# Score tiles of queries made by transposing DMAs, keys kept as their high part twice, and four moves in the order of a one-core transformer layer

## The chip, the cores and the metric

The kernel runs on one core of a Trainium2 chip. The metric is the device time of one execution in microseconds. The kernel before took 2648.01 us as the median of three runs (2645.45 to 2649.12). The core has five engines that run their own instruction streams in order and wait for each other by semaphores: TensorE (PE, with its weight loads shown apart as PEld), VectorE (DVE), ScalarE (ACT), GpSimd (POOL) and SyncE (SP), which here issues nearly all DMAs.

## The reference, cut to what matters

One layer over 2048 latent tokens of width 1024, with 256 context tokens, in f32:

```python
h = rmsnorm(x, norm1_g) * (1 + sc1) + sh1
rq, rk, rv, rg, aq, ak, av = split(h @ w_in)      # 4 x 512, 512, 128, 128
ret = chunkwise_retention(rope(rq), rope(rk), rv, both directions)
ret = groupnorm(ret) * silu(rg)
q = rope(rmsnorm(aq by heads))                    # 8 heads of 64
k = rope(rmsnorm(ak by heads))                    # 2 heads of 64, context keys ahead
att = softmax(q @ k.T / 8) @ v                    # 4 query heads share a key head
x = x + g1 * (concat(ret, att) @ w_out)
h2 = rmsnorm(x, norm2_g) * (1 + sc2) + sh2
x = x + g2 * (relu(h2 @ w_ff1) ** 2 @ w_ff2)
out = rmsnorm(x, final_norm_g)
```

## The kernel before, in words

Products that need more than f16 are made of three f16 products: each operand is split into a high part and the low rest, and high x high, high x low and low x high are summed in PSUM. A tile of tokens is 128 rows; there are 16 of latents and 2 of context, 18 of keys in all.

**Projection (0 to 603 us).** The list `units` is run through one step s at a time. A step multiplies one tile with one block of columns of `w_in` (lines 1192 to 1194, 24 products of 512 columns), then `run_step(s)` issues what other work was registered for that step by `do(s, part, fn)`, in the fixed order of `PARTS` (line 305): "hi", "evac", "turned", "low", "vec", "pool", "root", "aux", "turn", "load", "store". Work that follows a product is registered for the steps s + 1 to s + 7 (`post`, line 688 ff). Tiles come in two groups: group 0 is the context and latents 0 to 3; group 1 the other twelve. In group 1 the columns of retention keys (RK) and of attention keys and values (AKV) alternate, after them attention queries (AQ) and retention queries (RQ). In the same steps the kernel also reads the weights of later stages (tiles `wm`, `wmo`, `wor`, `wst`), for DVE to sum, scale and split.

A tile of queries is normed and rotated on DVE and POOL into `ys`, turned on PE at s + 4 (line 711: four transposes of 128x128 into the PSUM tile `psx`), its high part made by ACT (line 782) and its low part by DVE (line 785) into `qhl`, and stored at s + 6 to the scratch `aq` (line 789) with the head's dimensions in the partitions. A tile of keys: the rotated key goes into `kn`; ACT makes its high part `kh` (line 829), DVE the low part beside the key (line 832), PE turns both at once (line 837, s + 6), DVE casts the result into `ks` (line 842, s + 7), so `ks` holds the high part in partitions 0 to 63 and the low part in 64 to 127. The PSUM tiles `psx` are shared by these transposes and by those of the latents (line 480).

The latents of group 1 are prepared in group 0's last steps and after (lines 1228 to 1254): load at step b - 4, square on ACT at b - 2, root at b - 1, norm on DVE at b (line 466), then the transposes on PE at b (line 480), then a scale that frees the PSUM tile (line 485).

**Attention (603 to 1458 us).** Iterations k of some 1.48 us, 18 to a group of four query heads of one token tile, 32 groups. In each iteration the events registered by `on(k, phase, fn)` run phase by phase. A group is loaded 14 iterations ahead (`Group.load`, lines 157 to 164, four DMAs into `qr`), its largest scores are found by `piece` (lines 177 and 181) and DVE (line 190), and its scores are two products (lines 210 and 211). `piece` of the first groups runs already within the projection. Retention runs beside it: the forward states are updated chunk by chunk (`update`, line 1643) in two SBUF places of tag "sf", and each is stored (`keep_state`, line 1648). The backward states have two places of tag "sb", used after. `output_scales` (line 1759) finds the scales of the output product; its last eight instructions are registered one to an iteration.

**Feed-forward (1458 to 2647 us).** Jobs of 12 products each (lines 2071 to 2073) of sums of blocks; an item has seven forms of weights `w1f`, made by ACT (line 2047) and DVE (line 2053). The last token tile's remaining work waits in the list `rest`: two groups of four transposes (line 1865), two modulations (line 1870), two shifts (line 1875), two stores. After the products of each job `rest_steps(2)` issues two of them, and once the list is empty its two PSUM banks are given to the jobs.

Of the kernel before, what the change touches and what calls it, by code (L numbers as in the profile page):

```python
# [22 lines left out]
P = 128  # L23
# [33 lines left out]
def layer_kernel(ctx: ExitStack, tc: tile.TileContext, a: dict, out: bass.AP):  # L57
# [34 lines left out]
    aq_d = scratch("aq", NT, [P, 2, 4, P], F16)  # L92
# [56 lines left out]
    class Group:  # L149
# [7 lines left out]
        def load(self):  # L157
            pool, tag = (mq, "mb") if self.n % 4 < 2 else (qp, "qr")
            self.qr = pool.tile([P, 2, 4, P], F16, name="qr", tag=tag, bufs=2)
            q = self.qr.rearrange("p x (j e) t -> p x j e t", e=2)  # L160
            for e in range(2):
                src = aq_d[self.t][64 * e : 64 * e + 64, :, 2 * self.g : 2 * self.g + 2]
                nc.sync.dma_start(q[:64, :, :, e], src)
                nc.sync.dma_start(q[64:, :, :, e], src)
# [105 lines left out]
    with ExitStack() as st, tc.manual_schedule():  # L270
# [418 lines left out]
        def post(s, g, col, kind, i, x):  # L689
# [73 lines left out]
            elif col == C_AQ:  # L763
# [25 lines left out]
                do(s + 6, "store", lambda: nc.sync.dma_start(aq_d[i], x["z"]))  # L789
            else:  # L790
# [36 lines left out]
                def high():  # L827
                    x["kh"] = op.tile([P, 2, HD], F16, name="kh", tag="kh")
                    nc.scalar.activation(x["kh"], x["kn"][:, :, 0], AF.Copy)

                def low():
                    nc.vector.tensor_tensor(x["kn"][:, :, 1], x["kn"][:, :, 0], x["kh"], op=ALU.subtract)
# [9 lines left out]
                do(s + 7, "vec", lambda: nc.vector.tensor_copy(ks[:, :, row * P : (row + 1) * P], x["pt"][:, :2]))  # L842
# [389 lines left out]
        for n, tile_of in enumerate(GROUPS[1]):  # L1232
# [288 lines left out]
    for g in range(2):  # L1521
        nc.sync.dma_start(ks2[:64, g], ks[:64, g])
# [87 lines left out]
    def retention(k0):  # L1610
# [94 lines left out]
        for n, (d, c) in enumerate(todo):  # L1705
# [6 lines left out]
            if d == 0:  # L1712
                old, to, tag = ("f" if c == STATES else "s", c - 2), ("s", c - 1), "sf"
# [45 lines left out]
    def output_scales(k):  # L1759
# [20 lines left out]
        def scales():  # L1780
# [11 lines left out]
            for i, fn in enumerate(later):  # L1792
                on(k + 4 + i, "late", fn)
# [163 lines left out]
    output_scales(39)  # L1957
# [450 lines left out]
    with tc.manual_schedule():  # L2408
# [78 lines left out]
```

## Time and profile before

| | us |
|---|---|
| median of three runs | 2648.01 |
| the profiled execution | 2648.93 |
| its span | 2647.1 |
| PE busy | 2597.4 |
| DVE busy | 2048.4 |
| POOL busy | 1756.4 |
| ACT busy | 1504.0 |

The mean granted clock of TensorE over the execution was 0.997 of full speed. A row of a timeline gives the start and the duration in us, the engine, the line of the kernel, what is written and read, and in brackets how long the engine had idled before and what it waited for. DMA rows on SP show the issue; landing times stand apart.

### The profile page before, as it was taken

What the parts mean: (1) busy time and instruction counts of PE and PEld (TensorE: products, weight loads), DVE (VectorE), ACT (ScalarE), POOL (GpSimd) and SP (SyncE); (2) the same over time, 40 slices, a digit from 0 to 9 for tenths busy, and PEclk for the clock granted to TensorE, in tenths of its full rate; (3) what the DMA queues carried; (4) which work ended last, traced back from release to release, by engine and by line L of the source; (5) the groups of instructions that cost most, each with busy time, mean ns of one, the idle gap of its engine ahead of it and who ended that gap; (6) DMA issues with size and microseconds to landing.
All of it is one profiled execution on the core that took longest, in us unless ns stands there. A gap on an engine that the chain in (4) does not pass through costs nothing.

```text
span 2647.1 us, 45439 instructions
## 1 busy us (share of the span) xinstructions
PE 2597.4 (98%) x16617; PEld 1452.3 (55%) x16617; DVE 2048.4 (77%) x3098; ACT 1504.0 (57%) x2544; POOL 1756.4 (66%) x1451
## 2 busy tenths in 40 slices
PE   8999999998999999999999999999999999999998
PEld 5875555545666666666666444444444444444443
DVE  5788898667888888888887697889886656656686
ACT  3855343426877777888788576666665322222243
POOL 3644566545676668798887685677662666666686
PEclk9999999999999999999999999999999999999999
DMA  7876999737112123333322755777685757475453
GB/s 235 270 253 211 309 325 322 261 116 221 51 57 73 57 85 100 95 85 107 112 81 77 278 160 151 236 237 230 211 291 148 278 174 296 163 288 178 157 189 113
DMA packets 332903, 481.84 MB, mean 182 GB/s; under 512 B 90228, under 2 KB 200068, under 8 KB 328200
## 3 DMA queue, kind: packets, MB, share of 16 engines
q1 hardware_dynamic: 332664, 478.94, 54.9%
q8 instruction: 130, 2.13, 0.3%
q14 instruction: 93, 0.76, 0.1%
q10 hardware_dynamic: 16, 0.01, 0.0%
HBM read 321.89 MB, written 156.38 MB: 181 GB/s over the span
## 4 chain that ended last, share of the span: by engine, by line
PE 82%; DVE 6%; DMA 4%; ACT 4%; issue 2%; POOL 2%; SPq 0%; ACTq 0%; DVEq 0%; POOLq 0%
PE pd L2298 7%; PE pd L2300 7%; PE pd L2299 7%; PE pu L2071 7%; PE pu L2073 7%; PE pu L2072 7%; PE st L210 4%; PE o L245 4%; PE st L211 4%; PE pso L1193 4%; PE pso L1192 4%; PE pso L1194 4%; PE mp L177 3%; PE o L243 2%; PE bank L1835 2%; PE bank L1833 2%
## 5 line engine op out<-in xcount | busy, mean ns | idle before, releaser
L190 DVE TENSOR_REDUCE nm<-mp 128x1 f32<-128x512 f32 x558 | 377.5, 685 | 88.6 <-PE mp L177 82.9
L216 ACT ACTIVATE p<-st 128x512 f32<-128x512 f32 x576 | 341.4, 600 | 158.4 <-PE st L211 154.8
L227 POOL TENSOR_TENSOR plo<-p,phi 128x1024 f16<-128x1024 f32 x160 | 347.7, 2178 | 84.9 <-ACT phi L220 84.8
L2071 PE MATMUL pu<-hf,w1f 128*128 128x512 f16 x896 | 339.8, 379 | 0.6 <-DVE u L1870 0.6
L2072 PE MATMUL pu<-hf,w1f 128*128 128x512 f16 x896 | 339.8, 379 | 0.0
L2073 PE MATMUL pu<-hf,w1f 128*128 128x512 f16 x896 | 339.8, 379 | 0.0
L2298 PE MATMUL pd<-w,uf 128*128 128x512 f16 x896 | 339.6, 379 | 0.0
L2299 PE MATMUL pd<-w,uf 128*128 128x512 f16 x896 | 339.6, 379 | 0.0
L2300 PE MATMUL pd<-w,uf 128*128 128x512 f16 x896 | 339.6, 379 | 0.0
L2318 POOL TENSOR_TENSOR y<-y,d 128x512 f32<-128x512 f32 x128 | 210.4, 1646 | 146.9 <-ACT uf L2287 100.1
L220 ACT ACTIVATE phi<-p 128x1024 f16<-128x1024 f32 x288 | 305.2, 1060 | 0.0
L229 DVE TENSOR_TENSOR plo<-p,phi 128x512 f16<-128x512 f32 x256 | 237.6, 929 | 21.8 <-ACT phi L220 9.4
L243 PE MATMUL o<-wv,plo 128*128 128x65 f16 x2304 | 230.6, 193 | 0.0
L245 PE MATMUL o<-wv,phi 128*128 128x129 f16 x2176 | 228.9, 220 | 0.0
L210 PE MATMUL st<-qr,ks 128*128 128x512 f16 x576 | 218.3, 379 | 10.3 <-ACT p L216 7.9
L243 PEld LDWEIGHTS <-plo 128*128 128x128 f16 x2304 | 205.5, 98 | 29.3 <-issue 1.5
L2310 DVE SCALAR_TENSOR_TENSOR y<-pd,scy,y 128x512 f32<-128x512 f32 x160 | 116.8, 747 | 131.5 <-PE pd L2300 131.5
L211 PE MATMUL st<-qr,ks 128*128 128x512 f16 x576 | 218.5, 379 | 0.0
L2083 DVE TENSOR_TENSOR r<-pu,r 128x512 f32<-128x512 f32 x224 | 149.9, 683 | 82.8 <-PE pu L2073 57.7
L1192 PE MATMUL pso<-wf,h_l 128*128 128x512 f16 (+1 forms) x576 | 208.1, 361 | 0.0
L1194 PE MATMUL pso<-wf,h_l 128*128 128x512 f16 (+1 forms) x576 | 208.1, 361 | 0.0
L1193 PE MATMUL pso<-wf,h_l 128*128 128x512 f16 (+1 forms) x576 | 208.1, 361 | 0.0
(392 smaller groups left out, 6110.4 us busy)
## 6 DMA issues: line engine op xcount, KB each, us to landing
wm<-in_w_ff SPq DMA_DIRECT2D x64, 512.0 KB, 7.1
u<-r SPq DMA_DIRECT2D x128, 256.0 KB, 4.5
ur<-u SPq DMA_DIRECT2D x128, 256.0 KB, 5.8
y<-x SPq DMA_DIRECT2D x64, 512.0 KB, 6.0
wf<-w2f SPq DMA_DIRECT2D x112, 256.0 KB, 3.0
w<-wf SPq DMA_DIRECT2D x28, 1024.0 KB, 10.2
w1r<-in_w_ff SPq DMA_DIRECT2D x48, 512.0 KB, 5.4
x<-y SPq DMA_DIRECT2D x48, 512.0 KB, 2.6
```

What stands on the lines that cost most here:

```text
L190: nc.vector.tensor_reduce(dst, src, axis=AX.X, op=ALU.max, negate=True)
L211: mm(ps, ks2[:, self.g, k], q[:, 1], start=False, stop=True)
L216: nc.scalar.activation(self.p[kt // 2][:, kt % 2], self.s.pop(kt), AF.Exp, scale=HD**-0.5)
L227: nc.gpsimd.tensor_tensor(lo, p, hi, op=ALU.subtract)
L243: mm(o[:, : HD + 1], lo[:, i, c], v[:, : HD + 1], start=False, stop=False)
L245: mm(o, hi[:, i, c], v[:, :VW], start=False, stop=last)
L2071: mm(pu[hf, i], whi, hi, start=k == 0, stop=False)
L2072: mm(pu[hf, i], whi, lo, start=False, stop=False)
L2073: mm(pu[hf, i], wlo, hi, start=False, stop=k == 3)
L2298: mm(ps, u[:, 0, b], w[:, b, 0], start=b == 0, stop=False)
L2299: mm(ps, u[:, 0, b], w[:, b, 1], start=False, stop=False)
L2300: mm(ps, u[:, 1, b], w[:, b, 0], start=False, stop=b == 3)
```

## The change

1. Queries. ACT and DVE split the rotated queries where they lie, token-major in SBUF, and `aq` keeps them so: per head 64 columns of high and 64 of low part. The PE transposes of queries are gone. `Group.load` now issues two transposing DMAs in place of four plain ones.
2. Keys. ACT copies the key beside itself instead of making its high part, and DVE's subtraction before the transposes is gone. After them DVE casts both copies into `ks`, which so holds the high part twice, and subtracts it from the PSUM tile into a new tile `kl` (one buffer). A new store sends `kl` to a scratch; `ks2` is loaded from there.
3. The third forward state is written into a place of tag "sb".
4. `output_scales` begins one iteration sooner, and its last eight instructions go two to an iteration.
5. Latents of group 1 are squared, rooted and normed one step sooner.
6. The list `rest` is started after job 2 instead of after job 0.

```diff
         def load(self):
             pool, tag = (mq, "mb") if self.n % 4 < 2 else (qp, "qr")
             self.qr = pool.tile([P, 2, 4, P], F16, name="qr", tag=tag, bufs=2)
-            q = self.qr.rearrange("p x (j e) t -> p x j e t", e=2)
-            for e in range(2):
-                src = aq_d[self.t][64 * e : 64 * e + 64, :, 2 * self.g : 2 * self.g + 2]
-                nc.sync.dma_start(q[:64, :, :, e], src)
-                nc.sync.dma_start(q[64:, :, :, e], src)
+            for x in range(2):
+                nc.sync.dma_start(self.qr[:, x], aq_d[self.t][:, self.g], transpose=True)
...
-                do(s + 4, "turn", turn)
                 def high():
-                    x["z"] = op.tile([P, 2, 4, P], F16, name="qhl", tag="zs")
-                    nc.scalar.activation(x["z"][:, 0], x["pt"], AF.Copy)
+                    x["z"] = op.tile([P, 8, 2, HD], F16, name="qhl", tag="zs")
+                    nc.scalar.activation(x["z"][:, :, 0], heads(x["y"], 8), AF.Copy)
                 def low():
-                    nc.vector.tensor_tensor(x["z"][:, 1], x["pt"], x["z"][:, 0], op=ALU.subtract)
+                    nc.vector.tensor_tensor(x["z"][:, :, 1], heads(x["y"], 8), x["z"][:, :, 0], op=ALU.subtract)
...
-                def high():
-                    x["kh"] = op.tile([P, 2, HD], F16, name="kh", tag="kh")
-                    nc.scalar.activation(x["kh"], x["kn"][:, :, 0], AF.Copy)
-                def low():
-                    nc.vector.tensor_tensor(x["kn"][:, :, 1], x["kn"][:, :, 0], x["kh"], op=ALU.subtract)
+                def double():
+                    nc.scalar.activation(x["kn"][:, :, 1], x["kn"][:, :, 0], AF.Copy)
...
-                do(s + 4, "hi", high)
-                do(s + 5, "low", low)
+                def parts():
+                    pt, hi = x["pt"][:, :2], ks[:, :, row * P : (row + 1) * P]
+                    x["kl"] = op.tile([HD, 2, P], F16, name="kl", tag="kl", bufs=1)
+                    nc.vector.tensor_copy(hi, pt)
+                    nc.vector.tensor_tensor(x["kl"], pt[:HD], hi[:HD], op=ALU.subtract)
+                do(s + 4, "hi", double)
                 do(s + 6, "turn", turn_k)
-                do(s + 7, "vec", lambda: nc.vector.tensor_copy(ks[:, :, row * P : (row + 1) * P], x["pt"][:, :2]))
+                do(s + 7, "vec", parts)
+                do(s + 7, "store", lambda: nc.sync.dma_start(kl_d[:, :, row], x["kl"]))
...
             do(b - 4, "load", rows.load, 0)
-            do(b - 2, "hi", rows.square, 0)
-            do(b - 1, "hi", rows.root)
-            do(b, "vec", rows.norm, 0)
+            do(b - 3, "hi", rows.square, 0)
+            do(b - 2, "hi", rows.root)
+            do(b - 1, "vec", rows.norm, 0)
...
-        nc.sync.dma_start(ks2[:64, g], ks[:64, g])
+        nc.sync.dma_start(ks2[:64, g], kl_d[:, g].rearrange("d n t -> d (n t)"))
...
-                old, to, tag = ("f" if c == STATES else "s", c - 2), ("s", c - 1), "sf"
+                old, to, tag = ("f" if c == STATES else "s", c - 2), ("s", c - 1), "sb" if n == 2 else "sf"
...
-                on(k + 4 + i, "late", fn)
+                on(k + 4 + i // 2, "late", fn)
...
-    output_scales(39)
+    output_scales(38)
...
-                if phase == "pe" and rest:
+                if phase == "pe" and rest and k > 1:
                     rest_steps(2)
```

On SP, in a step of the projection where a tile of keys reaches its place: before, the order of issue was this (`kt` and `rk` are the stores of turned and plain retention keys, the others are loads, but for `wo`).

```order
L1051 DMA wo_189<-wof 128x2048
L721 DMA rtb<-in_ret_cs 128x256
L676 DMA atb<-in_att_cs 128x128
L916 DMA wm<-in_w_ff 128x1024
L1037 DMA wor<-in_w_out 128x1024
L745 DMA kt_157<-zs 128x512
L735 DMA rk_76<-ys 128x512
L369 DMA wmo<-in_w_mod 128x2x512
L930 DMA wm<-in_w_ff 128x1024
```

The same place after the change:

```order
L1053 DMA wo_190<-wof 128x2048
L719 DMA rtb<-in_ret_cs 128x256
L674 DMA atb<-in_att_cs 128x128
L918 DMA wm<-in_w_ff 128x1024
L1039 DMA wor<-in_w_out 128x1024
L844 DMA kl<-kl 128x1x128
L743 DMA kt_158<-zs 128x512
L733 DMA rk_76<-ys 128x512
L367 DMA wmo<-in_w_mod 128x2x512
L932 DMA wm<-in_w_ff 128x1024
```

The store of `kl` has come ahead of the two others and of the loads behind them.

On DVE, where the first latents of group 1 are prepared (each `x_l` has its own number; L466 is the norm, L485 the scale of a turned tile), before:

```order
L485 TENSOR_TENSOR x_l_1891<-psx,a_273 128x512 x2
L466 TENSOR_SCALAR x_l_1948<-x_l_1948,xy 128x1024
...
L541 TENSOR_TENSOR wlo<-wst,whi 128x1024 x3
L485 TENSOR_TENSOR x_l_1948<-psx,a_273 128x512 x2
L466 TENSOR_SCALAR x_l_2005<-x_l_2005,xy 128x1024
```

And after the change (line numbers are smaller by two):

```order
L483 TENSOR_TENSOR x_l_1878<-psx,a_274 128x512 x2
L464 TENSOR_SCALAR x_l_1999<-x_l_1999,xy 128x1024
...
L539 TENSOR_TENSOR wlo<-wst,whi 128x1024 x3
L483 TENSOR_TENSOR x_l_1938<-psx,a_274 128x512 x2
L464 TENSOR_SCALAR x_l_2049<-x_l_2049,xy 128x1024
```

After the first tile's scale now stands the norm of the third tile (1999), where the norm of the second (1948) stood before: every norm has moved up by one tile.

On DVE, at the start of attention, the updates of forward states (L1643, now L1645) between the maxima of scores (`wmx`), before:

```order
L1643 SCALAR_TENSOR_TENSOR sf<-sf,cd,bank_6894 128x128 x2
L190 TENSOR_REDUCE wmx<-mp 128x1
L229 TENSOR_TENSOR plo<-p_6847,phi 128x512
L1643 SCALAR_TENSOR_TENSOR sf<-sf,cd,bank_6894 128x128 x2
L190 TENSOR_REDUCE wmx<-mp 128x1
L229 TENSOR_TENSOR plo<-p_6847,phi 128x512
L1643 SCALAR_TENSOR_TENSOR sf<-sf,cd,bank_6947 128x128 x2
```

And after:

```order
L1645 SCALAR_TENSOR_TENSOR sb<-sf,cd,bank_6827 128x128 x2
L188 TENSOR_REDUCE wmx<-mp 128x1
L227 TENSOR_TENSOR plo<-p_6780,phi 128x512
L1645 SCALAR_TENSOR_TENSOR sb<-sf,cd,bank_6827 128x128 x2
L188 TENSOR_REDUCE wmx<-mp 128x1
L227 TENSOR_TENSOR plo<-p_6780,phi 128x512
L1645 SCALAR_TENSOR_TENSOR sf<-sb,cd,bank_6880 128x128 x2
```

The order is the same; the third state is written into another place, and the fourth reads it from there.

More of the change, by code (lines that the diff above doesn't have):

```diff
@@ L91, in layer_kernel @@
     rg_d = scratch("rg", NT, [P, 512])
-    aq_d = scratch("aq", NT, [P, 2, 4, P], F16)
+    aq_d = scratch("aq", NT, [P, 2, 4 * P], F16)
+    kl_d = dram.tile([HD, 2, NK, P], F16, name="kl", tag="kl")
     qt_d = scratch("qt", NT, [P, 512])
@@ L777, in post, with store @@
                 )
[L778 removed]
                 def high():
[L781 to L782 removed]
+                    x["z"] = op.tile([P, 8, 2, HD], F16, name="qhl", tag="zs")
+                    nc.scalar.activation(x["z"][:, :, 0], heads(x["y"], 8), AF.Copy)
                 def low():
[L785 removed]
+                    nc.vector.tensor_tensor(x["z"][:, :, 1], heads(x["y"], 8), x["z"][:, :, 0], op=ALU.subtract)
+                def store():
+                    nc.sync.dma_start(aq_d[i].rearrange("p g n -> p (g n)"), x["z"].rearrange("p h a d -> p (h a d)"))
                 do(s + 5, "turned", high)
                 do(s + 5, "vec", low)
[L789 removed]
+                do(s + 6, "store", store)
             else:
```

## The prediction

> **What bounds the kernel now.** I read the page's busy times and its chain first, then the busy time of each engine by stretch, then the idle gaps of TensorE (PE) row by row with what ended them.
>
> ```profile
> PE 2597.4 (98%) x16617; PEld 1452.3 (55%) x16617; DVE 2048.4 (77%) x3098; ACT 1504.0 (57%) x2544; POOL 1756.4 (66%) x1451
> PE 82%; DVE 6%; DMA 4%; ACT 4%; issue 2%; POOL 2%; SPq 0%; ACTq 0%; DVEq 0%; POOLq 0%
> ```
>
> PE is idle for only 2647.1 - 2597.4 = 49.7 us of the span, and it makes 82% of the chain that ended last. So time can be won in three ways: fewer PE instructions, shorter PE gaps, and stretches in which PE runs at its full clock. Columns of the next rows: busy us (instructions) of PE, PEld, DVE, ACT and POOL, then the granted PE clock, the DMA share and GB/s.
>
> ```profile
> 320.00:350.00 30.00, 30.00 (x194) 19.15 (x192) 29.42 (x44) 13.55 (x26) 20.99 (x27) 1.00 1.00 355
> 350.00:380.00 30.00, 26.07 (x161) 15.41 (x160) 25.80 (x33) 13.58 (x21) 16.07 (x19) 1.00 0.82 268
> 416.00:541.00 125.00, 122.00 (x642) 64.86 (x640) 93.09 (x152) 47.46 (x79) 76.71 (x78) 1.00 0.79 259
> ```
>
> While keys are projected PE, DVE and the DMA engines are all full (row one), and where loads come late all three sag together and PE idles 3.9 us (row two): here a saving on PE alone buys nothing, and work on DVE or a late load can cost. While twelve of the sixteen query tiles are projected (row three) PE is busy 122 of 125 us and DVE 93: here PE sets the pace.
>
> **The change, part by part.**
>
> *Queries.* The sixteen groups of four PE transposes go. What one costs:
>
> ```profile
> 468.66 0.38 PE L1194 MATMUL pso<-wf,h_l 128*128 128x512 f16 x1
> 468.87 0.60 PE L711 MATMUL psx<-ident,ys 128*128 128x128 f32 x4
> 469.31 0.38 PE L1192 MATMUL pso<-wf,h_l 128*128 128x512 f16 x1
> ```
>
> The product before takes 0.21 us until the transposes start, and these take 469.31 - 468.87 = 0.44 until the next product starts: sixteen cost 7.0. DVE's subtraction now reads SBUF twice in halves of 64 columns (the nearest row is h_l below, 0.81 us; at twice that, 26 us in all, it still fits into the 32 us of room that row three leaves DVE, less what the old form took). I take -6.5; the ends are 0 (something else paces the block) and -7.
>
> The loads go from four plain DMAs a group to two transposing ones, 64 instead of 128 in all. No transposing DMA is in the trace. The nearest rows:
>
> ```profile
> L210 PE MATMUL st<-qr,ks x576: 376/379/630, 603.4 to 1453.2; 128*128 128x512 f16 x192
> L163 SPq DMA_DIRECT2D qr<-aq x64: 573/612/1142, 453.2 to 1373.9; - x64
> L177 PE MATMUL mp<-ks,qr x512: 376/379/631, 459.3 to 1423.1; 128*128 128x512 f16 x171
> DMA to landing us min/median/max: 2.3/3.5/8.1
> ```
>
> An iteration of the attention lasts (1453.2 - 603.4)/575 = 1.478 us, and a group is loaded 14 iterations ahead: 20.7 us of cover against a median landing of 3.5 and a longest of 8.1. The very first group is issued at 453.2 and used at 459.3, 6.1 us. I take 0 for the loads; the ends are 0 and, if each transfer takes twice the longest landing (16 us), 10 us once, at the first group. The Trainium skill, "VectorE: DVE Perf Modes", section "The three transpose paths", gives 1309 ns for a 128x128 block by DMA against 390 ns on TensorE, and its rules prefer TensorE where the result may go to PSUM. By an estimate from that page the eight blocks of a group take 10.5 us one after the other: the sum would be some 4 us worse at the first group and no other. The row above says 0.44 us for four blocks, so here the page's price for TensorE is well above what is being saved.
>
> *Latents normalised a step sooner.* The PE gap that they cause:
>
> ```profile
> 174.76 3.50 DVE L541 TENSOR_TENSOR wlo<-wst,whi 128x1024 fp32r<-128x1024 f32 x3 [6.09 <-PE pso L1194]
> 178.18 1.28 DVE L485 TENSOR_TENSOR x_l<-psx,a 128x512 f32<-128x512 f32 x2
> 179.38 1.22 DVE L466 TENSOR_SCALAR x_l<-x_l,xy 128x1024 f32<-128x1024 f32 x1
> 180.74 1.48 PE L480 MATMUL psx<-ident,x_l 128*128 128x128 f32 x8 [2.00 <-DVE x_l L466]
> 181.00:185.00 4.00, 4.00 (x16) 3.37 (x15) 3.96 (x6) 3.48 (x7) 2.35 (x4) 0.57 0.00 0
> ```
>
> PE waits 2.00 us for the norm (L466), which stands behind three weight splits and the scale of the tile before. One step earlier the norm is done before the step's wait begins; what is late next is the scale (L485), which frees the PSUM tile: 178.18 + 1.28 = 179.46 against 178.74, when PE stopped (180.74 - 2.00), so 0.3 to 0.7 us stay. After the stall the granted clock is 0.57 over four microseconds, a loss of 1.7 us. I take -1.5 and -1.7 together, **-3.2**; without the clock it is -1.5. The Trainium skill, "TensorE: Matmul & The Clock Gate", section "Why this matters for your kernels", warns of PE-idle gaps of more than about 3 us; by it a gap of 2.00 costs no clock and this term would be -1.5. The trace differs: 0.57 stands right behind a gap of 2.00, and 0.66 behind one of 2.75 (below).
>
> *Third place for forward states.*
>
> ```profile
> 612.62 0.32 SPq L1648 DMA_DIRECT2D sf<-sf  x1
> 617.66 0.61 DVE L1643 SCALAR_TENSOR_TENSOR sf<-sf,cd,bank 128x128 f32<-128x128 f32 x2 [1.63 <-DMA sf<-sf]
> ...
> 627.39 0.61 DVE L1643 SCALAR_TENSOR_TENSOR sf<-sf,cd,bank 128x128 f32<-128x128 f32 x2 [1.62 <-DMA sf<-sf]
> 624.71 0.38 PE L181 MATMUL mp<-ks,qr 128*128 128x256 f16 x2 [2.75 <-DVE wmx L190]
> 624.00:629.00 5.00, 4.29 (x30) 3.47 (x30) 3.38 (x9) 0.87 (x2) 1.04 (x1) 0.66 0.93 305
> ```
>
> Between 617 and 628 us DVE waits three times, some 1.6 us each, for the store that last used the place (issued 612.62, awaited until 617.66: 5 us). With a third place for update 2, each update finds a place whose store is one chunk, about 5 us, older. The reductions behind these updates come sooner, the PE gap of 2.75 us goes or shrinks below 0.5, and the clock loss with it: (1 - 0.66) x 5 = 1.7. I take **-4**; the ends are -1.5 (the gap halves and the clock stays) and -5.
>
> *Last transposes two jobs later.*
>
> ```profile
> 1487.79 1.12 POOL L1860 TENSOR_SCALAR xr<-xr,cy_f 128x1024 f32<-128x1024 f32 x1 [11.73 <-DMA w1r<-in_w_ff]
> 1488.96 1.97 PE L1865 MATMUL bank<-ident,xr 128*128 128x128 f32 x8 [3.10 <-POOL xr L1860]
> 1488.00:1492.00 4.00, 3.04 (x12) 2.15 (x13) 1.35 (x2) 0.72 (x1) 4.00 (x4) 0.57 0.36 126
> 1489.74 0.75 DVE L2053 SCALAR_TENSOR_TENSOR w1f<-w1r,sc,w1f 128x512 f16<-128x512 f32 x1 [10.26 <-ACT w1f L2047]
> 1494.74 0.98 DVE L2053 SCALAR_TENSOR_TENSOR w1f<-w1s,sc,w1f 128x512 f16<-128x512 f32 x1 [3.65 <-ACT w1f L2047]
> 1497.98 1.28 DVE L2083 TENSOR_TENSOR r<-pu,r 128x512 f32<-128x512 f32 x2
> 1499.91 0.38 PE L2071 MATMUL pu<-hf,w1f 128*128 128x512 f16 x1 [0.64 <-DVE u L1870]
> ```
>
> PE waits 3.10 us, until the norm on POOL ends (1488.91), then loses 1.7 us of clock (0.57 over 4 us). Jobs 1 and 2 (24 products of 0.216, 5.2 us) use the last two forms of the first item, made before DVE's idle 10.26 us, and now run from 1485.86 to 1491.1, past the norm. Late next: job 3 needs a form that is made at 1490.5, which is in time, but job 4 needs the one made at 1494.74 + 0.98 = 1495.72 (about 0.6 us late) and job 5 a PSUM tile that DVE frees at 1498.6 (about 0.7 late). Before, job 4 lost 0.64 us. So 3.10 + 1.7 + 0.64 - 1.3 = 4.1, taken as **-4**; the ends are -2 and -5.2.
>
> *Keys, and the new store.* On PE nothing changes but four instructions' order. DVE loses one instruction per key tile and gains one:
>
> ```profile
> L832 DVE TENSOR_TENSOR kn<-kn,kh 128x128 f32<-128x128 f32 x18 | 7.7, 427 | 0.0
> L485 DVE TENSOR_TENSOR x_c<-psx,a 128x256 f32<-128x256 f32 x8 | 3.2, 421 | 1.2 <-PE psx L480 0.5 <-DVE a L359 0.5
> L495 DVE TENSOR_TENSOR h_l<-x_l,h_l 128x512 f16<-128x512 f32 x24 | 18.4, 807 | 0.0
> ```
>
> The new subtraction reads 256 columns of PSUM like the second row (0.42), the old took 0.43: 0 us a tile, or, where the old one ran undisturbed, 0.14 (2.5 us in 18). Its store is the matter. It stands ahead of the step's other stores on SP and waits for DVE:
>
> ```profile
> 315.27 0.33 SPq L745 DMA_DIRECT2D kt<-zs  x1
> ...
> 316.93 0.50 SPq L369 DMA_DIRECT2D wmo<-in_w_mod  x1
> 318.54 0.41 DVE L842 CAST ks<-psx 128x256 f16<-128x256 f32 x1
> 330.21 1.59 DVE L380 SCALAR_TENSOR_TENSOR macc<-wmo,cc,macc 128x512 f32<-128x512 f32 x2
> 359.71 0.38 SPq L916 DMA_DIRECT2D wm<-in_w_ff  x1
> 365.90 1.22 DVE L919 TENSOR_REDUCE wmx<-wm 128x1 f32<-128x1024 f32 x1 [3.08 <-DMA wm<-in_w_ff]
> wmo<-in_w_mod SPq DMA_DIRECT2D x14, 512.0 KB, 5.2
> wm<-in_w_ff SPq DMA_DIRECT2D x30, 512.0 KB, 8.1
> ```
>
> Here SP issued the key store at 315.27; now it first waits for the cast and the subtraction, 318.95 + 0.42 = 319.37, 4.1 us. Taken the same way, the twelve key tiles of this stretch are held 0 to 5.9 us each, 30 us in all. Behind it queue the stores of keys, then loads of weights, for which DVE waits in turn. The wmo load issued at 316.93 is the one that DVE adds up at 330.21, 13.3 us later against a landing of 5.2, so most of a hold is hidden; where the cover is short (the wm load of 359.71 is used 6.2 us later, and DVE waited 3.08 for it) it isn't. I take **+2**, two or three such places of about a microsecond, between 0 and, if every hold reaches DVE, +30.
>
> *Scales* of the output start one iteration sooner and end five sooner: 0 to within 0.5 us, hidden beside attention's products.
>
> **Sum.** -6.5 - 3.2 - 4 - 4 + 2 = -15.7 us. The profiled execution took 2648.93 us (span 2647.1), 0.9 above the median of the runs; 2648.0 - 15.7 = **2632.3**.
>
> **Rivals.**
>
> *The key store eats the gain.* For it: DVE is busy 29.4 of 30 us and the DMA engines are full exactly there, so DVE can't catch up what it loses; the subtraction's one buffer also makes DVE wait until the store before has landed. Against it: the cover just worked out. Price: from 0 to 30; at 30 the sum is -17.7 + 30 = +12, **2660**, slower. It decides when more than 17.7 of the 30 us of holds pass through to PE; with half (15) the time is within 0.2%.
>
> *Transposing loads miss their cover.* A group that lands L us after issue stalls PE by L - 20.7 in 31 groups. No row speaks for it, the landings of 2.3 to 8.1 speak against it. At L = 22 it is 31 x 1.3 = 40 us, less 15.7: **2672**. The milder form, in which only the first group comes late, is the 10 us above and ends at 2642.
>
> *The query block isn't PE's, and the stalls only move.* Then the transposes give little and the clock losses stay, or come at another place: 15.7 - 6.5 - 5.1 (three times 1.7) = 4, **2644**. For it: the 3.9 us of gaps between 350 and 380 cost no clock (1.00 in row two above), so the loss isn't set by a gap's length alone. Against it: 122 of 125. By the rule of the clock page above (the Trainium skill) the losses at the two shorter gaps are not the gaps' doing, and would stay.
>
> **How the numbers follow.** Forecast 0.70; key store 0.17 (0.02 still faster, 0.08 within, 0.07 slower); loads 0.06, slower; stalls move 0.07 (0.04 faster, 0.03 within). Measurement tells about 0.2%, 5.3 us, from no change. Faster 0.76, same 0.11, slower 0.13. The terms' good ends (-7, -3.7 with the whole gap, -5, -5.2, 0) give -21 and some 2627, with 2 for what wasn't seen 2625; upward I reach through the third rival and the key store's half, to 2650, which leaves out its bad end and the loads.
>
> **What would show it.** Right: no PE gap over 0.8 us near 179, 622 and 1486, a granted clock of 1.00 at all three places, and products 0.216 apart through the query tiles. The stretch from 290 to 440 us should be at most 3 us longer than before; if it is over 10 longer, with DVE waiting for wm or wmo, the key store was priced wrongly. A gap before the first pieces at 459 us or before pieces in attention that names the load of qr would show the transposing DMAs as slow.

## The result, and the profile after

The changed kernel took 2651.47 us as the median of 18 runs (2649.19 to 2658.55), the kernel before 2647.06 in the same session (18 runs, 2643.51 to 2650.13). The ratio is 1.0022 [1.0015, 1.0028]: **about 0.2% slower**, where 2632.3 us were forecast. The profiled execution of the change took 2656.05 us (span 2654.3), 4.6 above its median.

From the page of the change, its busy times:

```profile
PE 2597.4 (98%) x16553; PEld 1446.1 (54%) x16553; DVE 2051.9 (77%) x3098; ACT 1504.8 (57%) x2544; POOL 1763.0 (66%) x1451
```

PE issues 64 instructions less and is still busy for the same 2597.4 us, mostly because instructions at half clock last longer (past the start and before the end, half clock costs six times 1.7 us in this profile and three times in that of before); it now idles for 2654.3 - 2597.4 = 56.9 us, 7.2 more than before. To see in which stage, take the first and the last score product (the row of tile `st`, change):

```profile
L208 PE MATMUL st<-qr,ks x576: 376/379/630, 611.9 to 1461.2; 128*128 128x512 f16 x192
```

The projection ends 8.5 us later than before (611.9 against 603.4). Attention lasts 849.3 (before 849.8), and what follows 1193.1 (1193.9). The whole loss is in the projection, which was to become 7.7 us shorter (-6.5 - 3.2 + 2). There I read the granted clock (the last three columns are PE clock, DMA share and GB/s), in the change:

```profile
165.00:175.00 10.00, 7.80 (x33) 4.70 (x32) 6.67 (x17) 4.67 (x8) 4.03 (x5) 0.83 1.04 400
370.00:385.00 15.00, 10.99 (x45) 4.76 (x44) 14.41 (x20) 5.24 (x8) 7.23 (x10) 0.77 0.95 330
445.00:455.00 10.00, 6.87 (x26) 2.36 (x25) 9.86 (x14) 5.23 (x10) 6.13 (x6) 0.83 1.02 368
560.00:565.00 5.00, 4.29 (x16) 2.30 (x17) 3.32 (x14) 0.38 (x1) 0.00 (x0) 0.66 1.11 83
```

The clock costs 1.7 + 3.45 + 1.7 + 1.7 = 8.5 us there, against 1.7 in the profile of before. But this is one execution. An experiment below (kl_two_places) does the same work in the same median time, and its profile happened to catch a quicker execution (2647.54):

```profile
165.00:175.00 10.00, 7.90 (x39) 5.48 (x38) 7.01 (x19) 5.31 (x10) 4.53 (x6) 1.00 1.04 400
370.00:380.00 10.00, 6.63 (x25) 3.00 (x26) 9.59 (x12) 2.93 (x6) 3.53 (x3) 0.83 1.02 362
445.00:455.00 10.00, 8.76 (x46) 4.39 (x47) 9.90 (x15) 5.14 (x9) 7.97 (x8) 1.00 0.82 321
```

Its first score product:

```profile
L208 PE MATMUL st<-qr,ks x576: 376/379/379, 605.3 to 1450.1; 128*128 128x512 f16 x192
```

From 165 us on it loses 1.7 us of clock instead of 8.5, and its first score stands at 605.3 instead of 611.9. Lined up matmul by matmul, the two profiles drift apart by 1.6, 1.4, 1.6 and 1.7 us where the change alone has half clock, some 6.2 of the 6.6 us; the rest is drift both ways, half clock in the first 21 us of either included. So a profile pair must not be subtracted here without asking how many such windows each side caught. The gaps, on the other hand, are nearly the same in both, and they tell where the change loses. What SP's queue waited for in the change, from 90 to 460 us (columns: us in total, times, longest):

```profile
SPq L844 <- DVE kl L839: 16.4, 7, 5.8
SPq L844 <- DVE kn L646: 14.9, 5, 8.0
...
SPq L844 <- DMA wm<-in_w_ff: 3.0, 2, 2.4
```

The new store holds SP for 16.4 + 14.9 + 3.0 = 34 us; the prediction had 30 for the twelve tiles of group 1. All of SP's waits in this stretch together don't grow, though (224 us before, 213 in the change): much of the hold replaces waits that later entries of the queue had, and only what is late for its user can cost. Where it arrives, in the timeline of the change:

```profile
370.05 1.22 DVE L921 TENSOR_REDUCE wmx<-wm 128x1 f32<-128x1024 f32 x1 [2.60 <-DMA wm<-in_w_ff]
371.18 1.27 DVE L541 SCALAR_TENSOR_TENSOR wf<-wst,sci,wf 128x1024 f16<-128x1024 f32 x1
372.38 1.22 DVE L1050 TENSOR_TENSOR wof<-wor,wof 128x1024 f16<-128x1024 f32 x1
373.51 0.42 DVE L838 CAST ks<-psx 128x256 f16<-128x256 f32 x1
373.96 0.42 DVE L839 TENSOR_TENSOR kl<-psx,ks 64x256 f16<-64x256 f32 x1
374.41 0.54 SPq L844 DMA_DIRECT2D kl<-kl  x1
374.52 0.66 PE L833 MATMUL psx<-ident,kn 128*128 128x128 f32 x2 [4.01 <-DVE kl L839]
...
448.64 1.00 PE L709 MATMUL psx<-ident,ys 128*128 128x128 f32 x4 [3.13 <-DVE ys L646]
```

Read from the bottom of the first seven rows: PE waits 4.01 us for a PSUM tile. That tile is released by the new subtraction (373.96), which follows the cast; the cast follows three long instructions, the first of which waited 2.60 us for a weight load. The eighth row is a like wait 75 us on, at another turn of PE. Near 370 PE waited 1.86 before; near 448 there was no such gap.

### The profile page after: what moved, and what is told of

Same layout as the page of the kernel before. It is cut to its first block, busy times and chain, and to the rows that moved or that the text cites. A ratio compares the mean times of both kernels' runs of the same rounds, so it can differ in the third digit from the quotient of the medians.

```text
span 2654.3 us, 45157 instructions
## 1 busy us (share of the span) xinstructions
PE 2597.4 (98%) x16553; PEld 1446.1 (54%) x16553; DVE 2051.9 (77%) x3098; ACT 1504.8 (57%) x2544; POOL 1763.0 (66%) x1451
## 4 chain that ended last, share of the span: by engine, by line
PE 80%; DVE 6%; DMA 5%; ACT 4%; POOL 2%; issue 2%; SPq 0%; ACTq 0%; DVEq 0%; POOLq 0%
PE pd L2301 7%; PE pd L2302 7%; PE pd L2300 7%; PE pu L2073 7%; PE pu L2074 7%; PE pu L2075 7%; PE st L208 4%; PE o L243 4%; PE st L209 4%; PE mp L175 3%; PE pso L1194 3%; PE pso L1195 3%; PE pso L1196 3%; PE o L241 2%; PE bank L1837 2%
## 5 line engine op out<-in xcount | busy, mean ns | idle before, releaser
L208 PE MATMUL st<-qr,ks 128*128 128x512 f16 x576 | 218.3, 379 | 10.4 <-ACT p L214 7.9
```

## The experiments

Each is compared with the kernel before on its own chip; ratios below 1 are faster. "First score" is the length of the projection in that kernel's profile. Four profiles whose projection equals that of before put it at 601.5 to 603.4, mean 602.4.

### Each part alone

**Keys alone**: the change with parts 1 and 3 to 6 taken back.

> The kernel before with only the keys' part of the change (doubled key, subtraction after the turn, one-buffer kl, its store ahead of the step's others); its query loads stay as they were, so that its scores are about doubled. Theory A (the key store costs what the rest gains): the projection ends 8 to 12 us later, the whole is 8 to 12 us slower than before. Theory B (the keys' part costs what was forecast, and the other parts simply gain nothing): 0 to 3 us slower.

Measured: 2655.41 us, ratio 1.0034 [1.0021, 1.0046], first score 610.7. The keys alone lose more than the whole change does, and SP is held as long as there:

```profile
SPq L845 <- DVE kl L840: 17.2, 6, 5.5
SPq L845 <- DVE kn L649: 14.5, 5, 7.6
```

**Queries alone**: the query part in the kernel before, with the low keys copied from where they lie.

> The kernel before with only the queries' part: no transposes of queries on PE, transposing loads. Its second score product pairs the queries with the low parts of the keys in place of low queries with high keys. Theory A: the block of queries is PE's, so 5 to 7 us faster. Theory B (the saved PE time is lost to waits for DVE and ACT in the same block): within 2 us of before.

```diff
-        nc.sync.dma_start(ks2[:64, g], ks[:64, g])
+        nc.sync.dma_start(ks2[:64, g], ks[64:, g])
```

Measured: 2644.29 us, ratio 0.9992 [0.9984, 1.0001], first score 599.6. A gain of about 2, not 6.5, and not clear of no gain at all. Its timeline:

```profile
151.77 0.63 PE L708 MATMUL psx<-ident,ys 128*128 128x128 f32 x4 [0.88 <-DVE ys L645]
166.32 0.66 PE L708 MATMUL psx<-ident,ys 128*128 128x128 f32 x4 [1.66 <-DVE x_l L482]
547.31 0.69 ACT L696 ACTIVATE xs<-pso,sci 128x512 f32<-128x512 f32 x1 [6.35 <-DVE t L632]
548.33 1.13 PE L1159 MATMUL psf<-early 128*128 128x128 f32 x8 [2.69 <-issue]
```

The clock (0.83) in the ten microseconds around the last of these:

```profile
545.00:555.00 10.00, 7.30 (x30) 3.37 (x29) 6.55 (x19) 1.32 (x2) 1.05 (x1) 0.83 0.60 109
```

The same place in the timeline of the kernel before:

```profile
552.24 0.63 PE L711 MATMUL psx<-ident,ys 128*128 128x128 f32 x4 [0.44 <-DVE ys L650]
552.81 0.69 ACT L699 ACTIVATE xs<-pso,sci 128x512 f32<-128x512 f32 x1 [5.58 <-DVE t L635]
553.83 1.13 PE L1160 MATMUL psf<-early 128*128 128x128 f32 x8 [0.96 <-issue]
```

At the last query tile PE starts `psf` 0.33 us after ACT has emptied a PSUM bank in both kernels (548.00 and 553.50), and ACT waits for DVE. "Issue" is only the view's word for a wait that it can't name. Before, the turned queries filled part of that time; without them PE just waits 2.69 instead of 0.96 + 0.44, and a window of half clock follows (0.83 over ten, 1.7 us). In group 0 PE waits for DVE at two places: two gaps grow by 0.88 and 1.31 (none and 0.35 before). Together 1.3 + 1.7 + 2.2 = 5.2 of the 7.0 us saved are given back at three places that the prediction didn't look at. That is read from the timeline and not tried by a run of its own, and smaller gaps elsewhere move both ways (near 377 and 424 they shrink from 2.07 and 1.71 to 1.20 and none), so this sum closes only to a few microseconds.

**Latents alone**: part 5 of the change in the kernel before, three lines of its diff.

> The kernel before with only the latents of the second group normalised one step sooner. The gap of 2.0 us near 180 us should fall under 0.5. If clock loss follows such a gap in most executions: 3 us faster. If, as the four parts' profiles show, it followed in one of five: 1.5 to 2 us faster.

Measured: 2645.14 us, ratio 0.9991 [0.9982, 0.9999], first score 601.0:

```profile
180.18 1.23 PE L480 MATMUL psx<-ident,x_l 128*128 128x128 f32 x8 [0.27 <-DVE x_l L485]
```

The gap of 2.00 is 0.27, and what is late now is the scale (L485), as forecast. The gain is 1.4 by the medians, about the gap's part, but the interval reaches from 0.3 to 4.8. The granted clock, which is on record for every execution, averages 0.9981 here and 0.9974 in the kernel before on this chip, worth about 1.8 us by an estimate; at which place that clock is gained one profile can't tell. So whether this part gains 1.4 or the forecast 3.2 stays open.

**Forward states alone**: part 3, one line.

```diff
-                old, to, tag = ("f" if c == STATES else "s", c - 2), ("s", c - 1), "sf"
+                old, to, tag = ("f" if c == STATES else "s", c - 2), ("s", c - 1), "sb" if n == 2 else "sf"
```

> The kernel before with only the third place for forward states. If the three waits for the stores caused the PE gap of 2.75 us and its clock loss: 3 to 5 us faster, and no PE gap over 1 us between 615 and 630 us. If DVE's other work at that place sets it: under 1 us faster, and a gap of about 2 us stays while DVE no longer waits for a store.

Measured: 2643.97 us, ratio 0.9990 [0.9981, 0.9998]. The gap of 2.75 shrinks to 0.68; the second row stands earlier in the same timeline:

```profile
620.95 0.38 PE L181 MATMUL mp<-ks,qr 128*128 128x256 f16 x2 [0.68 <-DVE wmx L190]
...
181.90 1.06 PE L480 MATMUL psx<-ident,x_l 128*128 128x128 f32 x8 [2.00 <-DVE x_l L466]
```

And the clock behind that second row:

```profile
181.00:185.00 4.00, 3.10 (x18) 2.75 (x19) 3.96 (x5) 2.94 (x6) 3.23 (x4) 1.00 0.00 0
```

The gain is 2.4 by the medians, with 0.5 to 5.0 from the interval, so the forecast 4 is not excluded. The gap itself is not steady: in the five other profiles of kernels that leave the states as before, the gap before the products of `mp` at this place is 1.28, 1.63, 2.09, 2.10 and 2.92. The later two rows are for another question: this kernel's projection is that of before, with the same gap of 2.00 at the latents, and yet the clock behind it is 1.00. Six profiles hold that gap of 2.00 or 2.01 (before and five of the experiments); only that of before shows half clock behind it.

**Last transposes alone**: part 6, one line.

```diff
-                if phase == "pe" and rest:
+                if phase == "pe" and rest and k > 1:
```

> The kernel before with only the last transposes two jobs later. If the forecast's term holds: 4 us faster. If the wait of 2.6 us for the modulation of the last tile, seen in the changed kernel some 20 us after, belongs to this edit: the gap of 3.1 us and the clock loss go, a gap of 2 to 3 us comes at job 6, and the gain is 1.5 to 2.5 us.

Measured: 2647.21 us, ratio 1.0003 [0.9994, 1.0012]. The gap of 3.10 is gone, and these have come:

```profile
1490.68 0.39 PE L2073 MATMUL pu<-hf,w1f 128*128 128x512 f16 x1 [0.42 <-DVE w1f L2053]
1493.62 0.38 PE L2071 MATMUL pu<-hf,w1f 128*128 128x512 f16 x1 [0.61 <-DVE r L2083]
1497.94 0.38 PE L2071 MATMUL pu<-hf,w1f 128*128 128x512 f16 x1 [1.56 <-DVE u L1870]
```

In the change itself the third of them is 2.62. DVE and PE there:

```profile
1509.06 1.79 DVE L2055 SCALAR_TENSOR_TENSOR w1f<-w1s,sc,w1f 128x512 f16<-128x512 f32 x1
1511.37 1.27 DVE L1872 TENSOR_TENSOR u<-bank,a 128x512 f32<-128x512 f32 x2
1512.10 0.38 PE L2073 MATMUL pu<-hf,w1f 128*128 128x512 f16 x1 [2.62 <-DVE u L1872]
```

The two modulations (`u`) empty the two PSUM banks that the jobs get next. Two jobs later they stand on DVE behind the weights and squares of the later jobs, so the banks come late: 0.42 + 0.61 + 1.56 = 2.6 us in place of 3.10 + 0.64. This profile is the quickest of eleven executions (2641.73); in the six other profiles with this edit the largest gap at these jobs is 2.61 to 3.31, so most often the wait has only moved.

**Scales alone**: part 4, two lines.

```diff
-                on(k + 4 + i, "late", fn)
+                on(k + 4 + i // 2, "late", fn)
...
-    output_scales(39)
+    output_scales(38)
```

> The kernel before with only the output scales sooner and two to an iteration. Forecast of record: within 0.5 us of before. If DVE's two steps in one iteration delay the maxima: 1 us slower, with a gap of 1.7 to 1.9 us before the maxima at 635 us where 1.2 stood.

Measured: 2647.44 us, ratio 0.9999 [0.9988, 1.0010]. One place reacts, a wait of 1.16 before:

```profile
640.60 0.38 PE L177 MATMUL mp<-ks,qr 128*128 128x512 f16 x1 [1.89 <-DVE nm L190]
```

That is 0.7 us, too little for the ratio to show. A kernel without the scales (keys_two_copies, below) has 1.58 there, so not even all of it is theirs.

### The keys taken apart

All of these hold the change's other five parts unless said otherwise.

**Keys as before**, with part 2 taken back.

> The changed kernel without the keys' part (its second score product takes the keys' low parts in place of low queries with high keys). If the parts simply add, with what they measured alone (queries -2.1, states -2.4, last transposes +0.8) and some -2 for the latents: 4 to 7 us faster than before. If the parts other than the keys spoil each other: within 2 us of before.

```diff
-                do(s + 7, "vec", parts)
-                do(s + 7, "store", lambda: nc.sync.dma_start(kl_d[:, :, row], x["kl"]))
+                do(s + 7, "vec", lambda: nc.vector.tensor_copy(ks[:, :, row * P : (row + 1) * P], x["pt"][:, :2]))
...
-        nc.sync.dma_start(ks2[:64, g], kl_d[:, g].rearrange("d n t -> d (n t)"))
+        nc.sync.dma_start(ks2[:64, g], ks[64:, g])
```

Measured: 2640.93 us, ratio 0.9976 [0.9964, 0.9987], first score 600.0. The other five parts together gain 5.6 us (2646.57 was before on this chip).

**Two places for `kl`**, so that no subtraction waits for a store to land.

> The changed kernel with two places for kl (the two halves of the partitions, by turns), the store where it was. If DVE's wait for the store before (3.6 us in the changed kernel between 100 and 180 us, inside a single place) is what costs: 4 to 8 us faster than the changed kernel, that is faster than before. If SP's wait for DVE costs: within 2 us of the changed kernel, 4 us slower than before.

```diff
-                    x["kl"] = op.tile([HD, 2, P], F16, name="kl", tag="kl", bufs=1)
+                    if not kls:
+                        kls.append(op.tile([P, 2, P], F16, name="kl", tag="kl", bufs=1))
+                    x["kl"] = kls[0][HD * (row % 2) : HD * (row % 2) + HD]
```

Measured: 2651.28 us, ratio 1.0017 [1.0009, 1.0026]. It is as slow as the change: the single buffer, and DVE's wait for it, is not the cause.

**The store a step later**, with the two places.

> The changed kernel with two places for kl and its store one step later, so that neither DVE waits for the store nor SP for DVE. If one of these waits is what the keys' part costs: 6 to 10 us faster than the changed kernel, 2644 or less. If it is DVE's longer work on a key tile, or the bytes of the store: within 2 us of the changed kernel.

```diff
-                do(s + 7, "store", lambda: nc.sync.dma_start(kl_d[:, :, row], x["kl"]))
+                do(s + 8, "store", lambda: nc.sync.dma_start(kl_d[:, :, row], x["kl"]))
```

Measured: 2644.96 us, ratio 0.9993 [0.9985, 1.0002]. Same instructions on every engine, one line moved by one step, on the same chip 6.3 us less than with the store at s + 7. SP's waits at the store:

```profile
SPq L848 <- DVE kn L646: 5.5, 3, 4.6
SPq L848 <- DVE kl L843: 3.2, 2, 2.1
```

**One store in all**, of the last key tile's `kl` alone.

> The changed kernel with kl stored for the last key tile alone (17 of its 18 stores left out, and the low parts of that tile used for all). It keeps DVE's subtraction, the doubled key and the longer hold of the PSUM tile. Theory A (SP's wait before the store): as fast as without the keys' part, 2641 to 2643. Theory B (part of the cost is the longer hold of the PSUM tile and DVE's longer work, since with the store a step later 4 us of the cost stayed): 2644 to 2646.

```diff
-                do(s + 7, "store", lambda: nc.sync.dma_start(kl_d[:, :, row], x["kl"]))
+                if row == NK - 1:
+                    do(s + 7, "store", lambda: nc.sync.dma_start(kl_d, x["kl"]))
```

Measured: 2644.49 us, ratio 0.9987 [0.9978, 0.9996], first score 601.7. Seventeen stores fewer gain no more than holding SP less.

**One subtraction too**: besides the one store, the last tile's subtraction alone.

> The changed kernel with kl made and stored for the last key tile alone (17 of 18 subtractions and stores left out; that tile's low parts serve for all). Against the kernel with one store (2644.5, first score at 601.7): if DVE's subtraction after the turn, with the PSUM tile held for it, is what is left of the keys' cost: 2 to 4 us faster, 2641 to 2642.5, first score at 600. If the rest is the noise of the medians: within 1.5 us, 2643 to 2646.

```diff
-                    nc.vector.tensor_tensor(x["kl"], pt[:HD], hi[:HD], op=ALU.subtract)
+                    if row == NK - 1:
+                        x["kl"] = op.tile([HD, 2, P], F16, name="kl", tag="kl", bufs=1)
+                        nc.vector.tensor_tensor(x["kl"], pt[:HD], hi[:HD], op=ALU.subtract)
```

Measured: 2642.45 us, ratio 0.9978 [0.9969, 0.9987], first score 600.6. PE's wait near 370, first with all subtractions (keys_one_store):

```profile
370.04 0.41 PE L833 MATMUL psx<-ident,kn 128*128 128x128 f32 x2 [2.62 <-DVE kl L839]
```

and with one (keys_one_low):

```profile
366.24 0.44 PE L833 MATMUL psx<-ident,kn 128*128 128x128 f32 x2 [0.36 <-DVE ks L837]
```

Side by side, with PE's two waits of the timeline, DVE's waits for the loads of `wm` and `wmo` from 290 to 450 us, the half-clock time in the profile from 365 to 460 us, and the granted clock averaged over all executions of a kernel. The kernels ran on several chips, so the second column is the median less that of the kernel before on the same chip:

| kernel | median us | against before | PE near 370 | PE near 445 | DVE for loads | half clock | mean clock |
|---|---|---|---|---|---|---|---|
| no_keys | 2640.93 | -5.6 | 1.54 | none | 2.8 | none | 0.9973 |
| keys_one_low | 2642.45 | -5.2 | 0.36 | 2.14 | 2.7 | 3.4 | 0.9972 |
| keys_one_store | 2644.49 | -2.7 | 2.62 | 0.52 | 3.1 | 3.4 | 0.9966 |
| kl_store_later | 2644.96 | -1.6 | 3.18 | 1.76 | 3.7 | 3.4 | 0.9967 |
| kl_two_places | 2651.28 | +4.7 | 3.98 | 3.51 | 6.3 | 3.4 | 0.9957 |
| the change | 2651.47 | +4.4 | 4.01 | 3.13 | 6.2 | 10.2 | 0.9959 |

DVE's waits of the change, and after them that of no_keys:

```profile
DVE wmx L921 <- DMA wm<-in_w_ff: 4.9, 2, 2.6
DVE macc L378 <- DMA wmo<-in_w_mod: 1.3, 2, 1.1
```

```profile
DVE wmx L918 <- DMA wm<-in_w_ff: 2.8, 1, 2.8
```

The step from 2640.93 to 2651.28 (same chip) is 10.4 us. Of it 6.3 go with SP's hold, and DVE's late loads go with it (3.7 to 6.3). The other 4.0 come with the subtraction, its store and the longer use of the PSUM tile; here the two ratios' intervals overlap a little ([0.9964, 0.9987] and [0.9985, 1.0002]). Taking away subtractions as well (2644.49 to 2642.45) gives 2.0, or 2.5 against before on each chip, but these two intervals overlap more, so how those 4 us divide stays open.

Part of the 10.4 is lost as clock. In all seven profiles of kernels that subtract after the turn for every key tile, the wait at the key turn near 370 is 2.12 to 4.54 us and half clock follows it; in the other nine it is 1.86 or less and none follows it directly. Two profiles of the same chip, kl_store_later and then no_keys (PE's clock is the third column from the end):

```profile
370.00:380.00 10.00, 9.95 (x47) 4.79 (x48) 9.69 (x14) 5.23 (x8) 6.97 (x8) 0.83 0.96 294
370.00:380.00 10.00, 8.80 (x52) 4.63 (x51) 9.86 (x14) 5.46 (x10) 6.91 (x9) 1.00 0.99 333
```

The mean clocks of the table agree: from 0.9973 to 0.9967 and 0.9957 of some 2650 us is, by an estimate good to about 1 us, 1.8 us of the 4.0 and 2.5 of the 6.3.

### Other versions

**Four parts** (queries; keys with two places and the store at s + 8; states; latents), without scales and last transposes; and the same with the last transposes one job later:

> Queries, keys with kl in two places and its store one step later, states and latents; last transposes and scales as before. If the moves of scales and last transposes cost more than they bring beside the others (1.7 to 1.9 us before the maxima at 635 us, 4 to 5 us after job 3 against 3.6): 2 to 4 us faster than the kernel with all parts and the later store, so 2641 to 2643. If they are neutral: 2645.

> The same four parts, with the last transposes one job later instead of two. The gap of 3.1 us should fall to about 0.5, and the modulation comes one job sooner than in the changed kernel, so that the gap at the later job stays under 1.5 us: 1 to 2 us faster than the four parts. If each job of delay only moves the wait: equal to them within 1 us.

```diff
-                if phase == "pe" and rest:
+                if phase == "pe" and rest and k > 0:
```

Measured: 2644.47 us, ratio 0.9992 [0.9984, 1.0001], and 2645.41 us, 0.9998 [0.9989, 1.0007]. The last transposes bring nothing at one job's distance either: the gap of 3.53 at the transposes falls to 0.87, and one of 3.66 comes at a later job.

**Two copies**: queries, states and latents; the keys are made as before, and the high part is copied over the low one once, when the projection's keys are done. The diff, against the change, leaves out the lines that put part 2 back, as in no_keys:

> Queries, states and latents as in the change; keys as before (high and low part side by side), and between projection and attention two copies a group: the low parts into the second score tile, then the high parts over the low ones. No store of kl at all. The maxima found before pair low queries with low keys, which only moves the shift of the softmax. If the key store and the subtraction on DVE are what sank the change: as fast as without the keys' part or faster, 2639 to 2642, and faster than both kernels. If the copies are late for the first scores (two landings of about 6 us after 577): a PE gap before 600 us and 2644 or more.

```diff
     for g in range(2):
-        nc.sync.dma_start(ks2[:64, g], kl_d[:, g].rearrange("d n t -> d (n t)"))
+        nc.sync.dma_start(ks2[:64, g], ks[64:, g])
...
+    for g in range(2):
+        nc.sync.dma_start(ks[64:, g], ks[:64, g])
```

Measured: 2640.92 us, ratio **0.9973 [0.9963, 0.9982]**, faster than both kernels. The key layout that the transposing loads need costs two DMAs, with no wait of PE behind them ahead of the first score:

```profile
579.59 0.47 SPq L1524 DMA_DIRECT2D ks<-ks  x1
586.99 0.48 SPq L1524 DMA_DIRECT2D ks<-ks  x1
```

The first and the last score product there:

```profile
L207 PE MATMUL st<-qr,ks x576: 376/379/389, 599.8 to 1445.9; 128*128 128x512 f16 x192
```

## Why the prediction was wrong, step by step

The forecast was 19.2 us too low: 15.7 faster was forecast, 4.4 slower measured, and the kernel before itself ran 0.9 faster than in the three runs that the forecast started from. The keys' term was short by some 8.4 (10.4 for 2), the gains by some 12 (-17.7 forecast, -5.6 measured in no_keys). The largest single error, and the one that turned the sign, is the keys' term: with +2 for it the other parts as measured would still have made the kernel faster.

**Keys: the step that failed most.** The term was +2, "most of a hold is hidden"; it measured about 10.4. The mechanism of the first rival was at work, but at a fifth of its price (6.3 of 30). It decided all the same, because the gains that it had to eat were 5.6 and not 17.7; the other 4.0 came with the subtraction, its store and the longer use of the PSUM tile. Two things were missed. First, the holds were counted rightly (30 forecast, 34 measured in a longer stretch) and so was what of them reaches DVE: its waits for loads rose by 6.2 - 3.9 = 2.3 us against before (3.1 for wm and 0.8 for wmo there), "two or three such places of about a microsecond". But I stopped at DVE. DVE is full there, so each late load pushes its whole queue, and PE's turns, which need a PSUM tile back, wait at the end of it: 1.54 became 4.01 and none became 3.13, 5.6 us for 3.4 of load waits against no_keys, and half clock behind waits of that length comes on top. Second, the subtraction was priced by its length, 0.42 for 0.43 removed. It stands elsewhere: the old one was between two SBUF tiles, the new one sits between the cast and the release of the PSUM tile, where the rows show PE waiting for it; what this alone costs stays open. The sign that the prediction named for the key store, a stretch from 290 to 440 us that is over 10 us longer, did not come: the transposes of `early` (`psf`) that start at 437.0 before start at 439.3 in the change, and the key turn at 308.3 before starts at 310.1. The transposes of queries that are gone hide the loss near 370, and the second wait stands at 448, just behind the stretch.

**Queries: -6.5 forecast, -2.1 measured, with -4.2 to +0.3 from the interval.** The count (sixteen times 0.44) holds; that "PE sets the pace" was read from the middle of the block (122 of 125 us busy) and applied to all sixteen tiles. At two places of group 0 and at the last query tile PE waits for DVE or, through ACT, for DVE. The end that I had named, "something else paces the block", was right for these.

**Transposing loads: 0, right.** The row of the change, and the landings of its 64 loads:

```profile
L162 SPq DMA_TRANSPOSE qr<-aq x64: 1188/1262/2507, 460.2 to 1382.1; - x64
...
DMA to landing us min/median/max: 2.5/3.2/7.1
```

They land about as soon as the plain ones (median 3.2 here and 4.0 in queries_alone, 3.7 before; the prediction's 3.5 counted the sixteen stores of `aq` too), and no wait of PE names them. The estimate of 10.5 us a group from the Trainium skill's table ("VectorE: DVE Perf Modes", "The three transpose paths") is not borne out: the longest of all took 7.1 here and 7.6 in queries_alone, and the two of a group are issued 1.26 apart.

**Clock: three times 1.7 us booked from one profile.** The prediction read 0.57 behind the gap of 2.00 and booked its return as a gain. The same gap is followed by full clock in five other profiles, so as far as the profiles tell this term was an accident of one execution. At the forward states two of six profiles that leave them as before show the loss, behind gaps of 2.75 and 2.92, and four with gaps of 1.28 to 2.10 don't. At the last transposes the loss is nearly a property of the place: six of eight profiles that leave them as before show it, behind gaps of 2.85 to 3.53. There the mistake was another: the gap moved and the loss moved with it, as four of the six profiles with a moved gap of 2.61 to 3.31 show. By the medians, -3.2 for the latents was -1.4 (its gap part -1.5) and -4 for the states -2.4, and both forecasts lie inside the measured intervals. There the trace of before seemed to differ from the Trainium skill's rule of about 3 us ("TensorE: Matmul & The Clock Gate", "Why this matters for your kernels"); over six executions a gap of 2.00 mostly agrees with it, while gaps of 2.61 to 2.92 mostly don't (17 of 21 were followed by half clock). The third rival, which left these losses in place, was nearer on these terms than the forecast.

**Forward states in the change itself.** The wait for the store is gone there, yet a gap stands close by:

```profile
622.32 2.49 DVE L227 TENSOR_TENSOR plo<-p,phi 128x512 f16<-128x512 f32 x1
...
625.98 0.38 PE L175 MATMUL mp<-ks,qr 128*128 128x512 f16 x1 [2.28 <-DVE wmx L188]
```

One subtraction took 2.49 us in this execution, and the next maximum came late. In kl_two_places the same gap is 1.07 and in kl_store_later 0.94.

**Last transposes: -4 forecast, nothing measured.** Two late places were foreseen, 1.3 us in all; the third and largest, the banks behind `u`, was not, since the step was followed as far as the norm and the weights, not to what the moved work itself releases. The interval, 1.6 faster to 3.2 slower, leaves out the forecast's 4.

**Scales: 0 to within 0.5.** Not contradicted: the ratio tells no more than some 3 us either way.

Sum of the parts alone by their medians: +9.0 - 2.1 - 1.4 - 2.4 + 0.8 + 0.3 = +4.2, and the change measured +4.4 (2651.47 - 2647.06). Each is good to some 2 us, so the parts add up as far as can be told.

## What to carry to other kernels

A store in an in-order DMA queue is not priced by its bytes but by how long it waits for its producer and by what is queued behind it: put it where its data is surely ready, here one step later for 6.3 us, or do it once outside the crowded stage. Where an engine is full, follow a delay through it to whoever waits for its buffers, and don't stop at the engine. A loss that appears in a single profiled execution, such as a window of half clock, belongs in a sum only after other executions have shown it at the same place; where they do, as behind the key turn near 370, it belongs to the price.

## What the runs showed of the hardware

The loss of clock comes in pieces: past the start of a profile and before its end, half clock is always granted for 3.41 us or for two such stretches on end, so 1.7 us are lost (0.83 over ten us, 0.66 over five) or 3.4. A longer gap makes it likelier. Of all PE gaps of 1.5 us and more that lie between 30 us and the end in the 16 profiles, half clock began within 3.5 us of the gap's end, or was already running there, behind 3 of 42 gaps under 2.05 us, 7 of 14 from 2.05 to 2.4, and 29 of 36 of 2.6 and more. At one place: behind the gap of 2.00 at the latents it came in 1 of 6 profiles. Behind the gap of 2.69 or 2.70 at `psf`, which every kernel with the query part has, it came in 8 of 10; kl_two_places is one of the two without, here its gap and its clock:

```profile
555.80 1.13 PE L1166 MATMUL psf<-early 128*128 128x128 f32 x8 [2.70 <-issue]
```

```profile
550.00:560.00 10.00, 7.30 (x38) 3.65 (x37) 8.17 (x27) 0.69 (x1) 1.70 (x2) 1.00 0.56 68
```

A transposing DMA holds SP for 1.26 us at its issue, a plain one of the same tile 0.61 before. With 64 instead of 128 the time that SP spends on issuing them stays at some 80 us.
